# Joint steps for two query blocks of a key search and for two heads of a gated linear attention

## The chip, the cores and the metric

The kernel runs on one core of one Trainium2 chip. A core has a matrix engine (TensorE, PE in the profile), a vector engine (VectorE, DVE), a scalar engine (ScalarE, ACT), GpSimd (POOL) and a queue engine for DMAs (SyncE, SP). Each works through its own list of instructions in the order in which it was built, and waits on semaphores where an instruction needs what another engine makes. The metric is the device time of one execution, in microseconds (us); less is better.

## The reference

One layer of an encoder for 1024 tokens of width 1024, in float32: half a SwiGLU feed-forward step, a layer norm, a token mixer, a layer norm, another half feed-forward step, a layer norm. The mixer holds what the change touches:

```python
proj = h @ w_in                        # one projection, cut into groups of columns
# gated linear attention (GLA), 4 heads, in chunks: b is the running sum of the log gates
A = einsum('bhid,bhjd,bhijd->bhij', qn, kn, exp(b_i - b_j))   # causal
o = A @ v + (qn * exp(b)) @ S          # then a norm per head and a gate
# indexer attention (DSA), 8 heads: every query keeps its 256 best keys
score = einsum('bqh,bqhs->bqs', w, relu(q_idx . k_idx))       # admissible keys only
_, idx = lax.top_k(score, 256)
out = softmax over the kept keys
x = LN2(alpha * x + concat(o_gla, o_dsa) @ w_out)
```

## The kernel before

The mixer lies between the two feed-forward steps. Matrices are multiplied as a high and a low part, so each float32 product is three matmuls (L706 to L708, L723 to L725). A scheduler orders the instructions of each engine by a simulated timeline when the kernel is built; in the stretch below, the order of TensorE is pinned by hand (`in_order`, with a list that says how many projection steps follow each GLA step), while VectorE's, ScalarE's and GpSimd's follow from the simulation.

*Scores and search.* `index_scores` makes the scores of 128 queries (one block) against the keys up to them. Blocks 2 to 7 have more than 256 keys. `search_keys` finds each query's threshold bit by bit: a count of the scores above a trial threshold, a comparison of the count that gives 0 or a bit (`ge`), and a new threshold (`thr`), 32 times, one step waiting for the one before. Blocks 2 to 5 form one group: four counts on VectorE (L836), one comparison of four columns (L840), one update of four (L854). Blocks 6 and 7 are two groups of one block; their counts are ScalarE activations of 896 and 1024 columns (L833, with a row that reads the accumulator), their comparisons (L838) and updates (L852) single columns on VectorE. Then `keep_keys` turns a block's threshold into a mask on VectorE (L871 to L880; for blocks 6 and 7 `next_above`, L888 to L903, ahead of it); for blocks 5 and 6 it is held back until the third and fourth L1031.

*GLA.* `gla_pair` handles two of the four heads, pair 0 and then pair 1, and each in two halves of 512 tokens (i = 0, 1). A pair begins with the gates: pz by matmul (L937), L946, L951 and a running sum. A half begins with the diagonal: pd by matmul, then L1031 writes it into the tile `at` (128 x 1024). Then, for distances L = 64, 32, ..., 1, it scales keys and queries (ee by L1043, kz by GpSimd, qz by L1051), multiplies them (pa, L1057), and copies the result into `at` where a mask says so: on ScalarE for L = 64 (L1066), by a predicated copy for the others (L1068), once for each head. At last po = at · v + qe · state (L1082, L1085), the sum of squares (L1093, L1094) and the gated output og (L1098). The PSUM tiles pz, pd, pa and po come from two pools of two banks each, one per head.

*Beside it.* TensorE's time between GLA steps is filled with projections. In the second half of pair 1 these are `pf` (L706 to L708), each split by ScalarE (L1479) and VectorE (part, L1480) and sent to DRAM; two PSUM tiles take turns. After them attention begins (lg, L1149; e, L1153).

Of the kernel before, what the change touches and what calls it, by code (L numbers as in the profile page):

```python
# [7 lines left out]
F32 = mybir.dt.float32  # L8
# [107 lines left out]
class Block:  # L116
# [660 lines left out]
    def index_scores(self, b, parts, wI, ip, sp, ps, scores):  # L777

        nc = self.nc
        ik_hi, ik_lo, iq = parts  # L780
        n = (b + 1) * P
        sc = scores[b] = sp.tile([P, n], F32, name=f"score{b}")
        w = n if n <= 512 else n // 2
        for c0 in range(0, n, w):
            for h in range(8):
                pt = ps[h % 2].tile([P, 512], F32, tag="ps", name=self.uid("ps"))
                lhsT = iq[b // 4][h][:, b % 4 * P : (b % 4 + 1) * P]
                nc.tensor.matmul(pt[:, :w], lhsT, ik_hi[:, c0 : c0 + w], start=True, stop=False)
                nc.tensor.matmul(pt[:, :w], lhsT, ik_lo[:, c0 : c0 + w], start=False, stop=True)
                r = ip.tile([P, 512], F32, tag="relu", name=self.uid("relu"), bufs=2)  # L790
                nc.scalar.activation(r[:, :w], pt[:, :w], AF.Relu)
                if h == 0:
                    nc.vector.tensor_scalar(sc[:, c0 : c0 + w], r[:, :w], wI[:, b, 0:1], None, ALU.mult)
                else:
                    nc.vector.scalar_tensor_tensor(
                        sc[:, c0 : c0 + w], r[:, :w], wI[:, b, h : h + 1], sc[:, c0 : c0 + w], ALU.mult, ALU.add
                    )
                if h == 3:
                    yield
            yield  # L800
        nc.gpsimd.memset(sc[0:64, n - 64 : n], NEG)

    def search_keys(self, scores, keep, sp, tp):
# [12 lines left out]
        for gi, grp in enumerate(((2, 3, 4, 5), (6,), (7,))):  # L816
            s = {"blocks": grp, "act": gi >= 1, "id": gi, "n": (grp[-1] + 1) * P}
            t = keep.tile([P, 3, len(grp)], I32, name=f"search{gi}")
            s.update((k, t[:, j, :]) for j, k in enumerate(("ge", "thr", "cnt")))
            state.append(s)  # L820

        def count(s, value):

            count = s["cnt"].bitcast(F32)
            for j, b in enumerate(s["blocks"]):
                n = (b + 1) * P
                thr = s["thr"].bitcast(F32)[:, j : j + 1]
                cnt = count[:, j : j + 1]  # L830
                if s["act"]:
                    junk = tp.tile([P, 2 * T], BF16, tag="work", name=self.uid("junk"), bufs=1)
                    nc.scalar.activation(junk[:, :n], scores[b], AF.Sign, bias=thr, scale=-1.0, accum_out=cnt)  # L833
                else:
                    junk = sp.tile([P, s["n"]], U8, tag=f"junk{s['id']}", name=self.uid("junk"), bufs=1)
                    V.tensor_scalar(junk[:, :n], scores[b], thr, None, ALU.is_ge, ALU.add, accum_out=cnt)  # L836
            if s["act"]:
                V.tensor_scalar(s["ge"], count, float(s["n"] - 2 * TOPK + 1), value, ALU.is_le, ALU.mult)  # L838
            else:
                V.tensor_scalar(s["ge"], count, TOPK - 0.5, value, ALU.is_ge, ALU.mult)  # L840
# [6 lines left out]
        for p in range(30, -1, -1):  # L847
            for s in state:
                count(s, float(1 << p))
                xor = (ALU.bitwise_xor, ALU.bitwise_xor)  # L850
                if len(s["blocks"]) == 1:
                    V.tensor_scalar(s["thr"], s["thr"], turn[:, p : p + 1], s["ge"], *xor)  # L852
                else:
                    V.scalar_tensor_tensor(s["thr"], s["thr"], turn[:, p : p + 1], s["ge"], *xor)  # L854
# [52 lines left out]
    def gla_masks(self, pool):  # L907
# [9 lines left out]
        for s in range(6):  # L917
# [5 lines left out]
            masks[L] = self.const.tile([P, HP // L, L], U8, name=f"mask{L}")  # L923
# [3 lines left out]
    def gla_pair(self, p, g, gp, go, sgp, ps, masks, consts, o_dram):  # L927
# [6 lines left out]
        mz = kz  # L934
        for i in range(2):
            pz = ps[0].tile([P, 512], F32, tag="ps", name=self.uid("pz"))
            nc.tensor.matmul(  # L937
                pz,
                wa2[R_GA : R_GA + 16, p * P : (p + 1) * P],
                mT[R_GA : R_GA + 16, i * HT : (i + 1) * HT],  # L940
                start=True,
                stop=True,
                tile_position=(R_GA, 0),
            )
            nc.scalar.activation(az[i], pz, AF.Abs, bias=ba[:, p : p + 1], scale=1.0)
            V.tensor_scalar(mz[i], pz, ba[:, p : p + 1], 0.0, ALU.add, ALU.min)  # L946
# [60 lines left out]
        for i in range(2):  # L1007
# [6 lines left out]
            at = go.tile([P, 4, 2, P], F32, tag="at", name=self.uid("at"), bufs=1)  # L1014
            for step, L in enumerate((0, 64, 32, 16, 8, 4, 2, 1)):
# [7 lines left out]
                if L == 0:  # L1023
                    qk = kz[1]
                    nc.gpsimd.tensor_mul(qk, gk[:, ts], gq[:, ts])
                    pd = ps[0].tile([P, 8], F32, tag="ps", name=self.uid("pd"))
                    for j in range(4):
                        nc.tensor.matmul(
                            pd[:, 2 * j : 2 * j + 2], qk[:, j * P : (j + 1) * P], heads, start=True, stop=True
                        )  # L1030
                    V.tensor_mul(  # L1031
                        at.rearrange("p j h i -> p (j h) i"),
# [19 lines left out]
                pa = [t.tile([P, 4, HP], F32, tag="ps", name=self.uid("pa")) for t in ps]  # L1052
                m = HP if L == HP else P
                for j in range(4):
                    for h in range(2):
                        rows = slice(h * 64, h * 64 + 64)
                        nc.tensor.matmul(  # L1057
                            pa[h][:m, j, :],
# [5 lines left out]
                for h in range(2):  # L1064
                    if L == HP:
                        nc.scalar.activation(at[:HP, :, h, HP:], pa[h][:HP], AF.Copy)  # L1066
                    else:
                        V.copy_predicated(  # L1068
                            at[:, :, h, :].rearrange("p a (n s l) -> p a n s l", s=2, l=L)[:, :, :, 1, :],
                            masks[L].unsqueeze(1).to_broadcast([P, 4, HP // L, L]),  # L1070
                            pa[h].rearrange("p a (n l) -> p a n l", l=L),
                        )
# [3 lines left out]
            po = [t.tile([P, 4, P], F32, tag="ps", name=self.uid("po")) for t in ps]  # L1076
            for j in range(4):
                b = 4 * i + j
                tk = slice(j * P, (j + 1) * P)
                for h in range(2):  # L1080
                    vcols = slice(h * P, (h + 1) * P)
                    nc.tensor.matmul(po[h][:, j, :], at[:, j, h, :], gv[:, b, vcols], start=True, stop=(b == 0))  # L1082
# [151 lines left out]
    def run(self):  # L1234
# [15 lines left out]
        with tc.tile_pool(name="masks", bufs=1, reuse_waits="tile") as mkp:  # L1250
            masks = self.gla_masks(mkp)
# [169 lines left out]
        with ExitStack() as s2:  # L1421
# [8 lines left out]
            with ExitStack() as s3:  # L1430
                mp = s3.enter_context(tc.tile_pool(name="mix", bufs=1, reuse_waits="tile"))
                ps = [
                    s3.enter_context(tc.tile_pool(name=f"ps_mix{i}", bufs=2, space=PSUM, reuse_waits="tile"))
                    for i in range(2)
                ]
# [9 lines left out]

                s4 = ExitStack()
                ip = [s4.enter_context(tc.tile_pool(name="idx0", bufs=1, reuse_waits="tile"))]
# [44 lines left out]
                with s4:  # L1492
                    self.index_weights(mT, wI, 1)
                    side = dk_items()
                    for b in range(4, NB):
                        for _ in range(2):
                            next(side)
                        for _ in self.index_scores(b, parts, wI, ip[2], sp, ps, scores):
                            pass
                tp = s3.enter_context(tc.tile_pool(name="topk", bufs=1, reuse_waits="tile"))  # L1500
# [94 lines left out]
                for b in scores:  # L1595
# [74 lines left out]
        with ExitStack() as st, ExitStack() as ff_stack:  # L1670
# [3 lines left out]
            gb = xp.tile([P, 4, KD], F32, name="ln2_gb")  # L1674
# [116 lines left out]
```

## Time and profile before

| | |
|---|---|
| median of three runs | 1987.3 us (1987.25 to 1990.45) |
| profiled execution | 1987.65 us, span 1985.9 us |
| granted TensorE clock, mean of the span | 0.991 |
| busy: TensorE, VectorE, ScalarE, GpSimd | 97%, 76%, 42%, 32% |
| search and GLA pair 0 | about 811 to 964 us |
| GLA pair 1 | about 960 to 1092 us |

The profiled execution is 1.75 us longer than its span, which is what lies around the profile's first and last instruction. A row of the groups gives line, engine, operation, what is written and read, the shapes, the count, then busy time and mean nanoseconds of one, then the idle time of the engine ahead of it with what ended it. A row of the waits gives who waited for whom, the total, the number and the longest. A row of the timeline gives start, length, engine, line and operation, with idle time ahead of it in brackets. A length runs to the end of the instruction; the next one on the same engine can start a little earlier.

### The profile page before, as it was taken

Reading aid. Unit: us, or ns where it says so; the run is one execution under the profiler, and the core shown is the slowest. Engines: PE = TensorE matmul, PEld = TensorE weight load, DVE = VectorE, ACT = ScalarE, POOL = GpSimd, SP = SyncE. Lnnn points to the kernel's source line nnn. Section 1 sums busy time; section 2 is a strip of 40 time slices with the busy share of each in tenths; the row PEclk is TensorE's granted clock in tenths of the full one; section 3 lists DMA queues with packets and bytes.
Section 4 is the critical chain, followed back from the end, with each engine's and each line's share of the span. In section 5 each row is a group of like instructions: output and inputs, shape, how many; then the busy total and the mean of one; then the engine's idle time right before and its main releaser. Section 6 shows DMA issues by size and latency. Waiting matters only on the chain. (4 is left out here: it accounts for less than half of the span.)

```text
span 1985.9 us, 26695 instructions
## 1 busy us (share of the span) xinstructions
PE 1933.7 (97%) x9576; PEld 1584.2 (80%) x9576; DVE 1514.1 (76%) x2325; ACT 838.4 (42%) x1380; POOL 644.3 (32%) x531
## 2 busy tenths in 40 slices
PE   9999999999999999999899899999999999999996
PEld 7788888888888788777687678788888888888885
DVE  8777877775578768899967567478778878868677
ACT  5333323334334345798552456255332332234331
POOL 5454454430001102144343000025445444539011
PEclk9999999999999999998999899999999999999998
DMA  5454454478656222022115631523444534586663
GB/s 180 145 190 148 148 186 152 146 245 313 201 170 209 96 85 85 22 65 64 43 37 179 183 96 39 182 105 111 143 149 158 176 133 150 184 294 236 223 203 136
DMA packets 198309, 298.44 MB, mean 150 GB/s; under 512 B 18832, under 2 KB 102944, under 8 KB 198176
## 3 DMA queue, kind: packets, MB, share of 16 engines
q1 hardware_dynamic: 194272, 291.49, 44.8%
q10 hardware_dynamic: 3264, 3.15, 0.5%
q0 software_dynamic: 640, 2.10, 0.4%
q8 instruction: 75, 1.23, 0.3%
q14 instruction: 58, 0.48, 0.1%
HBM read 205.97 MB, written 90.70 MB: 149 GB/s over the span
## 5 line engine op out<-in xcount | busy, mean ns | idle before, releaser
L97 DVE TENSOR_TENSOR wloq<-rw,whiq 128x512 fp32r<-128x512 f32 (+2 forms) x211 | 212.9, 1010 | 126.2 <-ACT whiq L96 124.9
L97 DVE TENSOR_TENSOR wlod<-rd,whid 128x1024 fp32r<-128x1024 f32 x154 | 203.5, 1342 | 112.8 <-ACT whid L96 112.4
L96 ACT ACTIVATE whid<-rd 128x1024 fp32r<-128x1024 f32 x154 | 161.3, 1060 | 238.3 <-PE pd L543 122.1
L96 ACT ACTIVATE whiq<-rw 128x512 fp32r<-128x512 f32 (+2 forms) x211 | 164.2, 798 | 207.3 <-POOL rw L351 99.6
L543 PE MATMUL pd<-wlod,whid 128*128 128x512 f32 x616 | 239.6, 389 | 0.8 <-DVE wlod L97 0.8
L543 PE MATMUL pd<-whid,wlod 128*128 128x512 f32 x616 | 239.3, 389 | 0.0
L543 PE MATMUL pd<-whid 128*128 128x512 f32 x616 | 237.9, 390 | 0.0
L369 PE MATMUL pq<-b_h,whiq 128*128 128x512 f32 x576 | 226.3, 393 | 2.3 <-DVE c L418 1.8
L371 PE MATMUL pq<-b_h,wloq 128*128 128x512 f32 x576 | 225.5, 391 | 0.5 <-DVE wloq L97 0.5
L370 PE MATMUL pq<-b_l,whiq 128*128 128x512 f32 x576 | 225.4, 391 | 0.0
L228 POOL TENSOR_TENSOR rs<-ve,neghalf 128x1 f32<-128x1 f32 x24 | 34.2, 1427 | 473.9 <-DVE ve L252 322.1
L483 ACT ACTIVATE c<-c 128x512 f32<-128x512 f32 x80 | 50.7, 634 | 269.3 <-DVE c L405 182.3
L370 PE MATMUL pq<-xl,whiq 128*128 128x512 f32 x352 | 137.3, 390 | 0.6 <-DVE xl L97 0.6
L371 PE MATMUL pq<-xh,wloq 128*128 128x512 f32 x352 | 137.1, 389 | 0.0
L369 PE MATMUL pq<-xh,whiq 128*128 128x512 f32 x352 | 137.1, 389 | 0.0
L543 PEld LDWEIGHTS pd<-wlod,whid 128*128 128x128 f32 x616 | 115.7, 188 | 24.9 <-DVE wlod L97 1.1
L543 PEld LDWEIGHTS pd<-whid,wlod 128*128 128x128 f32 x616 | 115.6, 188 | 24.3
L543 PEld LDWEIGHTS pd<-whid 128*128 128x128 f32 x616 | 115.6, 188 | 23.9 <-ACT whid L96 0.2
L723 PE MATMUL pt<-whi,xh 128*128 128x512 f32 x320 | 131.0, 410 | 3.2 <-ACT stage L1550 1.6
L369 PEld LDWEIGHTS pq<-b_h,whiq 128*128 128x128 f32 x576 | 108.3, 188 | 26.6 <-DVE c L418 2.2
L371 PEld LDWEIGHTS pq<-b_h,wloq 128*128 128x128 f32 x576 | 108.1, 188 | 24.6 <-DVE wloq L97 1.0
L725 PE MATMUL pt<-whi,xl 128*128 128x512 f32 x320 | 127.7, 400 | 0.0
(275 smaller groups left out, 4533.8 us busy)
## 6 DMA issues: line engine op xcount, KB each, us to landing
rw<-in_ffn_w_gu_dram SPq DMA_DIRECT2D x87, 512.0 KB, 4.1
rd<-h_dram SPq DMA_DIRECT2D x154, 256.0 KB, 3.6
h_dram<-c SPq DMA_DIRECT2D x148, 256.0 KB, 2.9
rt<-in_ffn_w_down_dram SPq DMA_DIRECT2D x44, 512.0 KB, 3.4
t_dram<-rt SPq DMA_DIRECT2D x44, 512.0 KB, 2.9
rd<-t_dram SPq DMA_DIRECT2D x88, 256.0 KB, 3.7
rd<-in_ffn_w_down_dram SPq DMA_DIRECT2D x66, 256.0 KB, 4.8
raw<-in_w_in_dram SPq DMA_DIRECT2D x20, 512.0 KB, 3.7
```

The costliest lines, as they stand in the source:

```text
L96: self.nc.scalar.activation(hi, src, AF.Copy)
L97: self.nc.vector.tensor_sub(lo, src, hi)
L228: self.nc.gpsimd.tensor_tensor(dst, src, self.neghalf[:, :n], ALU.pow)
L369: mm(bank, wh[:, k, :], xh[:, k, :], start=start, stop=False)
L370: mm(bank, wh[:, k, :], xl[:, k, :], start=False, stop=False)
L371: mm(bank, wl[:, k, :], xh[:, k, :], start=False, stop=stop)
L483: nc.scalar.activation(t, t, AF.Silu)
L543: nc.tensor.matmul(bank, left, right, start=(i == 0 and n == 0), stop=(i == ng - 1 and n == 2))
L723: nc.tensor.matmul(pt, xh[:, k, cols], wh[:, k % 2, :], start=(k == 0), stop=False)
L725: nc.tensor.matmul(pt, xl[:, k, cols], wh[:, k % 2, :], start=False, stop=(k == KD - 1))
```

## The change

In the search, blocks 6 and 7 become one group on ScalarE. Its counts are both 1024 columns wide: block 6's score tile gets 128 more columns that GpSimd fills with the lowest value. A step is then two counts, one comparison and one update of two columns. In the GLA, both heads' PSUM tiles become one tile of two banks, from a pool of two such tiles, and `at` is laid out by head first; the copy of L = 64 on ScalarE and the predicated copies on VectorE take both heads at once (512 columns, 24 copies for 48). pz, too, is one tile for both halves, with both matmuls ahead of the steps that read it. The scores get a PSUM pool of their own that is closed before the GLA's opens. The masks are built at the mixer's start and kept in its pool, not at the program's start.

VectorE then has 2102 instructions for 2191 and ScalarE 1228 for 1234; TensorE has the same 8886, of which those of pair 0 stand in another order among the projections. The lines from `search_keys` on are numbered 3 to 5 higher: L836, L838, L840, L852 and L854 become L841, L843, L845 and (both) L856; L1031, L1057, L1068, L1098 and L1480 become L1035, L1062, L1072, L1103 and L1483.

```diff
-        sc = scores[b] = sp.tile([P, n], F32, name=f"score{b}")
+        sc = sp.tile([P, T if b == 6 else n], F32, name=f"score{b}")
+        scores[b] = sc[:, :n]
+        if b == 6:
+            nc.gpsimd.memset(sc[:, n:], NEG)
+            scores["wide", b] = sc
...
-        for gi, grp in enumerate(((2, 3, 4, 5), (6,), (7,))):
+        for gi, grp in enumerate(((2, 3, 4, 5), (6, 7))):
             s = {"blocks": grp, "act": gi >= 1, "id": gi, "n": (grp[-1] + 1) * P}
-            t = keep.tile([P, 3, len(grp)], I32, name=f"search{gi}")
+            t = keep.tile([P, 4, 4], I32, name=f"search{gi}")[:, :3, : len(grp)]
...
-                    nc.scalar.activation(junk[:, :n], scores[b], AF.Sign, bias=thr, scale=-1.0, accum_out=cnt)
+                    wide = scores["wide", 6] if b == 6 else scores[b]
+                    nc.scalar.activation(junk[:, :T], wide, AF.Sign, bias=thr, scale=-1.0, accum_out=cnt)
...
-                if len(s["blocks"]) == 1:
-                    V.tensor_scalar(s["thr"], s["thr"], turn[:, p : p + 1], s["ge"], *xor)
-                else:
-                    V.scalar_tensor_tensor(s["thr"], s["thr"], turn[:, p : p + 1], s["ge"], *xor)
+                V.scalar_tensor_tensor(s["thr"], s["thr"], turn[:, p : p + 1], s["ge"], *xor)
...
-            masks[L] = self.const.tile([P, HP // L, L], U8, name=f"mask{L}")
+            masks[L] = kept.tile([P, HP // L, L], U8, name=f"mask{L}")
...
+        pair = ps.tile([P, 2, 512], F32, tag="ps", name=self.uid("pz"))
         for i in range(2):
-            pz = ps[0].tile([P, 512], F32, tag="ps", name=self.uid("pz"))
             nc.tensor.matmul(
-                pz,
+                pair[:, i, :],
                 wa2[R_GA : R_GA + 16, p * P : (p + 1) * P],
                 mT[R_GA : R_GA + 16, i * HT : (i + 1) * HT],
                 start=True,
                 stop=True,
                 tile_position=(R_GA, 0),
             )
+        for i in range(2):
+            pz = pair[:, i, :]
...
-            at = go.tile([P, 4, 2, P], F32, tag="at", name=self.uid("at"), bufs=1)
+            at = go.tile([P, 2, 4, P], F32, tag="at", name=self.uid("at"), bufs=1)
...
-                    pd = ps[0].tile([P, 8], F32, tag="ps", name=self.uid("pd"))
+                    pd = ps.tile([P, 2, 512], F32, tag="ps", name=self.uid("pd"))[:, 0, :8]
...
-                pa = [t.tile([P, 4, HP], F32, tag="ps", name=self.uid("pa")) for t in ps]
+                pa = ps.tile([P, 2, 512], F32, tag="ps", name=self.uid("pa"))[:, :, : 4 * HP]
+                pa = pa.rearrange("p h (a l) -> p h a l", a=4)
...
-                for h in range(2):
-                    if L == HP:
-                        nc.scalar.activation(at[:HP, :, h, HP:], pa[h][:HP], AF.Copy)
-                    else:
-                        V.copy_predicated(
-                            at[:, :, h, :].rearrange("p a (n s l) -> p a n s l", s=2, l=L)[:, :, :, 1, :],
-                            masks[L].unsqueeze(1).to_broadcast([P, 4, HP // L, L]),
-                            pa[h].rearrange("p a (n l) -> p a n l", l=L),
-                        )
+                if L == HP:
+                    nc.scalar.activation(at[:HP, :, :, HP:], pa[:HP], AF.Copy)
+                else:
+                    V.copy_predicated(
+                        at.rearrange("p h a (n s l) -> p h a n s l", s=2, l=L)[:, :, :, :, 1, :],
+                        masks[L].unsqueeze(1).unsqueeze(1).to_broadcast([P, 2, 4, HP // L, L]),
+                        pa.rearrange("p h a (n l) -> p h a n l", l=L),
+                    )
...
-            po = [t.tile([P, 4, P], F32, tag="ps", name=self.uid("po")) for t in ps]
+            pair = ps.tile([P, 2, 512], F32, tag="ps", name=self.uid("po"))
+            po = [pair[:, h, :].rearrange("p (j f) -> p j f", j=4) for h in range(2)]
...
-        with tc.tile_pool(name="masks", bufs=1, reuse_waits="tile") as mkp:
-            masks = self.gla_masks(mkp)
...
-                ps = [
-                    s3.enter_context(tc.tile_pool(name=f"ps_mix{i}", bufs=2, space=PSUM, reuse_waits="tile"))
-                    for i in range(2)
-                ]
...
+                with tc.tile_pool(name="masks", bufs=1, reuse_waits="tile") as mkp:
+                    masks = self.gla_masks(mkp, mp)
...
+                ps = s4.enter_context(tc.tile_pool(name="ps_idx", bufs=4, space=PSUM, reuse_waits="tile"))
...
+                ps = s3.enter_context(tc.tile_pool(name="ps_gla", bufs=2, space=PSUM, reuse_waits="tile"))
...
-                for b in scores:
+                for b in range(TOPK // P, NB):
```

More of the change, by code (lines that the diff above doesn't have):

```diff
@@ L785, in index_scores @@
             for h in range(8):
-                pt = ps[h % 2].tile([P, 512], F32, tag="ps", name=self.uid("ps"))
+                pt = ps.tile([P, 512], F32, tag="ps", name=self.uid("ps"))
                 lhsT = iq[b // 4][h][:, b % 4 * P : (b % 4 + 1) * P]
@@ L903, in next_above, with gla_masks @@
         V.copy_predicated(tau, more, low)
-    def gla_masks(self, pool):
+    def gla_masks(self, pool, kept):
         nc = self.nc
@@ L1025, in gla_pair @@
                     nc.gpsimd.tensor_mul(qk, gk[:, ts], gq[:, ts])
-                    pd = ps[0].tile([P, 8], F32, tag="ps", name=self.uid("pd"))
+                    pd = ps.tile([P, 2, 512], F32, tag="ps", name=self.uid("pd"))[:, 0, :8]
                     for j in range(4):
                         nc.tensor.matmul(
-                            pd[:, 2 * j : 2 * j + 2], qk[:, j * P : (j + 1) * P], heads, start=True, stop=True
+                            pd[:, j::4], qk[:, j * P : (j + 1) * P], heads, start=True, stop=True
                         )
                     V.tensor_mul(
-                        at.rearrange("p j h i -> p (j h) i"),
+                        at.rearrange("p h j i -> p (h j) i"),
                         self.ident.unsqueeze(1).to_broadcast([P, 8, P]),
@@ L1057, in gla_pair @@
                         nc.tensor.matmul(
-                            pa[h][:m, j, :],
+                            pa[:m, h, j, :],
                             kk[rows, j * P : j * P + m],
@@ L1081, in gla_pair @@
                     vcols = slice(h * P, (h + 1) * P)
-                    nc.tensor.matmul(po[h][:, j, :], at[:, j, h, :], gv[:, b, vcols], start=True, stop=(b == 0))
+                    nc.tensor.matmul(po[h][:, j, :], at[:, h, j, :], gv[:, b, vcols], start=True, stop=(b == 0))
                 if b > 0:
@@ L1673, in run @@
             lp = ln_stack.enter_context(tc.tile_pool(name="ln2", bufs=1, reuse_waits="tile"))
-            gb = xp.tile([P, 4, KD], F32, name="ln2_gb")
+            gb = xp.tile([P, P], F32, name="ln2_gb")[:, : 2 * KD].rearrange("p (i k) -> p i k", i=2)
             self.affine = [gb[:, i, :] for i in range(2)]
```

## The prediction

> **What bounds the kernel now.** I read the page's first rows, then the busy time of each engine in stretches of 50 us, then the waits of TensorE in the stretches that are not full.
>
> ```profile
> span 1985.9 us, 26695 instructions
> PE 1933.7 (97%) x9576; PEld 1584.2 (80%) x9576; DVE 1514.1 (76%) x2325; ACT 838.4 (42%) x1380; POOL 644.3 (32%) x531
> ```
>
> TensorE (PE) is busy for 97% of the span. No row above changes its instructions, so the time can move only through its 52 us of gaps and through its clock. The stretches say where those lie (columns: stretch, length, then busy us and count of PE, PEld, DVE, ACT and POOL, the granted clock, the DMA share, GB/s):
>
> ```profile
> 850.00:900.00 50.00, 46.16 (x272) 36.89 (x271) 48.81 (x153) 45.23 (x79) 25.21 (x29) 0.93 0.21 64
> 900.00:950.00 50.00, 45.66 (x303) 37.61 (x302) 49.28 (x163) 42.50 (x88) 23.52 (x27) 0.93 0.25 75
> 950.00:1000.00 50.00, 43.93 (x218) 33.64 (x216) 48.85 (x105) 24.72 (x53) 16.92 (x17) 0.97 0.12 32
> 1000.00:1050.00 50.00, 48.50 (x320) 39.60 (x320) 31.60 (x61) 26.54 (x55) 25.35 (x29) 1.00 0.21 69
> ```
>
> From 850 to 1000 us VectorE (DVE) is full, at 48.8 to 49.3 us in 50, and TensorE lacks 3.8, 4.3 and 6.1 us. That is the search beside the first GLA pair and the entry of the second. From 1000 us VectorE has 18 us in 50 to spare and TensorE runs nearly without a stop. TensorE's longer waits from 850 to 1104 us:
>
> ```profile
> PE lg L1149 <- DVE mx L1153: 6.7, 1, 6.7
> PE pa L1057 <- DVE qz L1051: 4.0, 4, 1.5
> PE pa L1057 <- DVE at L1031: 3.9, 2, 2.6
> PE po L1082 <- DVE at L1068: 2.7, 1, 2.7
> PE pf L706 <- DVE part L1480: 1.4, 1, 1.4
> ```
>
> The wait at L1031 has its longest case at the entry of pair 1, that at L1480 in the second half of pair 1, and that of 6.7 us where attention begins.
>
> **The change part by part.** The durations of what is removed (groups of VectorE, then of ScalarE, from 811 to 1100 us; mean ns of one after the busy time):
>
> ```profile
> L1068 DVE COPY_PREDICATED at<-mask,pa 128x256 f32<-128x256 uint8 x48 | 23.1, 540 | 6.5 <-PE pa L1057 6.5
> L852 DVE TENSOR_SCALAR search<-search,turn 128x1 int32<-128x1 int32 x62 | 16.6, 269 | 0.0
> L838 DVE TENSOR_SCALAR search<-search 128x1 int32<-128x1 f32 x64 | 9.5, 149 | 4.8 <-ACT junk L833 4.5
> L854 DVE SCALAR_TENSOR_TENSOR search<-search,turn 128x4 int32<-128x4 int32 x25 | 7.9, 316 | 0.3
> L833 ACT ACTIVATE junk<-score,search 128x1024 bf16<-128x1024 f32 x32 | 36.7, 1145 | 9.0 <-DVE search L852 3.5 <-DVE search L838 3.2 <-POOL score L801 2.1
> L833 ACT ACTIVATE junk<-score,search 128x896 bf16<-128x896 f32 x31 | 32.2, 1038 | 3.2 <-DVE search L852 1.8 <-DVE search L838 1.2
> ```
>
> *VectorE's saving.* 64 of L838 become 32 of two columns, at the same 0.149 each: 4.8 us. 62 of L852 become 31 of L854's kind, at 0.316 or less: 16.6 − 9.8 = 6.8 us. Ends of these overlap the next start, so some 8 of the 11.6 us count as time. The joint copy of 512 columns has no row. If a copy's 0.540 were all fixed, 24 of 48 would save 13 us; if it were all by the column, nothing. Consecutive pairs below lie in 0.65 us (52.39 to 53.04), hence 0.33 from start to start; the nearest row with 512 columns, L1480 below, takes 0.60 (1049.80 to 1050.40). So I take 0.6 for a joint copy and 0.05 to 0.1 saved per pair, 1 us in pair 0. So pair 0's VectorE work falls by 9 us, with 5 and 15 as the ends.
>
> [...]
>
> *ScalarE.* 32 counts are widened by 128 columns: 32 × 0.108 = 3.5 us, less a few table loads. By its busy time (42%) this is nothing. But before, blocks 6 and 7 were two groups that took turns: while VectorE made the next threshold of one, ScalarE counted the other. Now both counts wait for one threshold and both must end before the next. The end of the search before:
>
> ```profile
> 948.37 1.05 ACT L833 ACTIVATE junk<-score,search 128x896 bf16<-128x896 f32 x1 [0.39 <-DVE search L838]
> 949.55 1.15 ACT L833 ACTIVATE junk<-score,search 128x1024 bf16<-128x1024 f32 x1
> 950.61 0.19 ACT L833 ACTIVATION_READ_ACCUMULATOR junk<-score,search 128x1 f32 x1
> 963.41 0.22 DVE L854 SCALAR_TENSOR_TENSOR search<-search,turn 128x4 int32<-128x4 int32 x1
> 992.50 1.21 DVE L1031 TENSOR_TENSOR at<-ident,pd 128x1024 f32<-128x1024 f32 x1
> ```
>
> ScalarE was done with its 32 steps at 950.8 us, 12.8 us ahead of VectorE's own group (963.6). A round of the new group is two counts (948.37 to 949.55 and 949.55 to 950.8, the first 0.1 longer at 1024 columns: 2.5 us) and two small VectorE steps (0.15 + 0.3): 2.9 us. VectorE's order at the end of the search, where L843 is the comparison (L838 before) and L856 the new threshold (L852, L854 before) of search_8698, the ScalarE group, and search_8697 is VectorE's own:
>
> ```order
> L841 TENSOR_SCALAR junk_9203,search_8697<-score_6060,search_8697 128x768
> L856 SCALAR_TENSOR_TENSOR search_8698<-search_8698,turn 128x2
> L845 TENSOR_SCALAR search_8697<-search_8697 128x4
> L856 SCALAR_TENSOR_TENSOR search_8697<-search_8697,turn 128x4
> L843 TENSOR_SCALAR search_8698<-search_8698 128x2
> L856 SCALAR_TENSOR_TENSOR search_8698<-search_8698,turn 128x2
> L1072 COPY_PREDICATED at_7335<-mask_5190,pa_7505 128x512
> ```
>
> L843 and L856 then follow four times more. Before, the same place held only VectorE's own group, and the keys of block 2 (L871) came straight after its last threshold:
>
> ```order
> L836 TENSOR_SCALAR junk_9327,search_8757<-score_6063,search_8757 128x768
> L840 TENSOR_SCALAR search_8757<-search_8757 128x4
> L854 SCALAR_TENSOR_TENSOR search_8757<-search_8757,turn 128x4
> L871 TENSOR_SCALAR keep_9339,above_9340<-score_5570,search_8757 128x384
> L872 TENSOR_SCALAR keep_9339<-score_5570,search_8757 128x384
> ```
>
> Five rounds of ScalarE's group stand after VectorE's last own threshold, with hardly any work between: the last copy of pair 0 after the first of them, one L950 (0.66 us, L946 before) before the last. VectorE takes them in order and waits at each. Its own group ends about 963.6 − 9 (saved) − 5 × 0.45 (steps still to come) = 952.4 us. The copy comes after one wait of 2.1 us and two steps, near 955.6 us, about where it stood before; so TensorE's 2.7 us for it (po at L1068) stays. Then the other rounds last until 952.4 + 2.6 + 4 × 2.9 = 966.6, and the keys of block 2 begin 3.0 us later than the 963.6 of before, with 0.7 us of later work done: L1031 of pair 1 ends about 2 us later. TensorE waits for it already (2.6), so **+2 us**, from −4 (15 us saved) to +6 (5 saved). All of VectorE's saving goes into waits for ScalarE.
>
> [...]
>
> *A move that the diff doesn't show.* In the second half of pair 1 TensorE computes projections (pf), each in one of two PSUM tiles, and the third must wait until VectorE's L1480 (L1483 in the changed kernel) has read the first. VectorE before, from 1037 us, with TensorE's row under it:
>
> ```profile
> 1037.09 1.22 DVE L1031 TENSOR_TENSOR at<-ident,pd 128x1024 f32<-128x1024 f32 x1 [0.55 <-PE pd L1028]
> 1043.63 2.15 DVE L1098 SCALAR_TENSOR_TENSOR og<-po,grs,gg 128x128 f32<-128x128 f32 x8
> 1045.70 0.67 DVE L1480 TENSOR_TENSOR part<-pf,part 128x512 fp32r<-128x512 f32 x1
> 1046.30 0.20 DVE L903 COPY_PREDICATED_SCALAR search<-na_more,na_low 128x1 f32 x1
> 1046.42 0.59 DVE L1051 TENSOR_TENSOR qz<-gq,ee 128x256 f32<-128x256 f32 x1
> 1046.94 0.68 DVE L1043 TENSOR_TENSOR ee<-bT 128x512 f32<-128x512 f32 x1
> 1047.54 1.13 DVE L871 TENSOR_SCALAR_CACHE_REDUCE keep<-score,search 128x896 f16<-128x896 f32 x1
> 1048.60 0.68 DVE L872 TENSOR_SCALAR keep<-score,search 128x896 f16<-128x896 f32 x1
> 1049.20 0.68 DVE L1043 TENSOR_TENSOR ee<-bT 128x512 f32<-128x512 f32 x1
> 1049.80 0.68 DVE L1480 TENSOR_TENSOR part<-pf,part 128x512 fp32r<-128x512 f32 x1
> 1050.40 0.14 DVE L874 TENSOR_SCALAR left<-above 128x1 f32<-128x1 f32 x1
> 1050.46 2.01 DVE L875 TENSOR_TENSOR_SCAN keep<-one,keep 128x896 f16<-128x896 f16 x1
> 1052.39 0.75 DVE L1068 COPY_PREDICATED at<-mask,pa 128x256 f32<-128x256 uint8 x2
> 1053.04 0.41 DVE L1051 TENSOR_TENSOR qz<-gq,ee 128x256 f32<-128x256 f32 x1
> 1053.37 1.14 DVE L876 SCALAR_TENSOR_TENSOR keep<-keep,left 128x896 f16<-128x896 f16 x1
> ```
>
> ```profile
> 1046.43 0.50 PE L706 MATMUL pf<-xh,whi 128*128 128x512 f32 x1 [1.41 <-DVE part L1480]
> ```
>
> The second head's og and the keys of block 6 stood behind L1480 or just ahead of it in the order before:
>
> ```order
> L1098 SCALAR_TENSOR_TENSOR og_8214<-po_8176,grs_8221,gg_7619 128x128 x4
> L1098 SCALAR_TENSOR_TENSOR og_8229<-po_8177,grs_8236,gg_7619 128x128 x4
> L1480 TENSOR_TENSOR part_8258<-pf_8169,part_8257 128x512
> L903 COPY_PREDICATED search_8758<-na_more_9389,na_low_9387 128x1
> L1051 TENSOR_TENSOR qz_6514<-gq_7616,ee_8370 128x256
> ```
>
> In the changed order, with the same steps renumbered (L1103 is og, L905, L1055, L1047 and L873 to L878 are L903, L1051, L1043 and L871 to L876), they stand between the first og and L1483:
>
> ```order
> L1103 SCALAR_TENSOR_TENSOR og_8169<-po_8132,grs_8176,gg_7589 128x128 x4
> L1047 TENSOR_TENSOR ee_8360<-bT_7562 128x512
> L905 COPY_PREDICATED search_8698<-na_more_9263,na_low_9261 128x1
> L1055 TENSOR_TENSOR qz_6516<-gq_7586,ee_8321 128x256
> L873 TENSOR_SCALAR keep_9266,above_9267<-score_6230,search_8698 128x896
> L874 TENSOR_SCALAR keep_9266<-score_6230,search_8698 128x896
> L877 SCALAR_TENSOR_TENSOR keep_9266<-one,keep_9266 128x896
> L1099 TENSOR_SCALAR ss_8183<-ss_8183 128x4
> L878 SCALAR_TENSOR_TENSOR keep_9266<-keep_9266,left_9270 128x896
> L1103 SCALAR_TENSOR_TENSOR og_8184<-po_8132,grs_8191,gg_7589 128x128 x4
> L1483 TENSOR_TENSOR part_8213<-pf_8125,part_8212 128x512
> ```
>
> All that stood behind L1480 from 1046.30 to 1052.39, less the 0.60 of the second L1480, is now ahead: 5.5 us; with it L876, some 1.1 us of its 1.14. That is 6.6 us. The second og needs a GpSimd step on ss that now lies right ahead, so up to 0.7 us more. TensorE's own order there is as before, and it already waited 1.41 us: **+6.9 us**, with 6.2 and 7.6 as ends; nothing earlier moves it, since VectorE's L1031 starts the count and itself waits for TensorE (0.55).
>
> A wait of over 8 us has a second cost, read from the stretch after the longest wait of before:
>
> ```profile
> 1099.00:1103.00 4.00, 3.96 (x15) 2.68 (x16) 2.06 (x15) 2.65 (x11) 0.00 (x0) 0.50 0.31 122
> 1103.00:1108.00 5.00, 5.00 (x37) 3.75 (x38) 3.73 (x23) 3.08 (x13) 0.00 (x0) 0.79 0.23 65
> ```
>
> The granted clock was 0.50 for 4 us and 0.79 for 5: 3.0 us lost. Part of it hides, as VectorE is then the later one for the next PSUM tile: the keys of block 7 stand ahead of the third L1483. I take **+2.3 us**, from 1 to 3.
>
> *Attention.* Its first reduction waited 5.4 us for a DMA out of kz, since its buffer shared addresses with kz; the moved masks shift it clear, but the second head's still overlaps. Three small matmuls can go ahead: **−1 us**, from 0 to −2. The masks' build now falls where VectorE idles before a weight arrives (about 440 us), at nothing; had it no cover it would cost some 2 us. The padding of block 6 is one GpSimd memset.
>
> Sum: +2 + 6.9 + 2.3 − 1 = +10.2 us on the profiled 1987.65 us, which is 0.35 over the median: 1987.3 + 10.2 = 1997.5 us.
>
> **The rivals.** *The saving holds (faster).* VectorE is full from 850 to 1000 us; if ScalarE's group kept pace, L1031 of pair 1 would come 9 us earlier. TensorE could use at most its waits there, 14.2 us, and would take about 9, so 1978; with the projection's wait in place 1986. It decides if a round takes under 2 us; against it stand two counts at 1.15. *A tie.* The two waits lie as forecast but the low ends meet: 15 us saved before the five rounds (−4), 6.2 at L1483, 1 for the clock, −2 at attention: +1.2, so 1988.5. For it: VectorE's saving has no row of its own, and 13 of the 15 us would need copies whose cost is all fixed; the spacing of 0.33 speaks against that. *More than I forecast.* The five rounds cost 3.4 us each instead of 2.9, and block 7's keys hold the third L1483 by 3 us too: +6, 2003. *The change doesn't do what it says*: joint copies could run as two halves, 24 × 0.1 = 2.4 us more on VectorE; it lies inside the ends above.
>
> **How the numbers follow.** Chances: forecast 0.68 (1992 to 2001 by its own ends), more than that 0.12, tie 0.12, faster 0.08. The likeliest gives 1997.5 us. The range reaches from 1986 (the saving holds, with the projection's wait) to 2004 (the upper case). A measurement of this kernel can tell about 0.2%, 4 us, from no change. So faster 0.08, same 0.12, slower 0.80.
>
> **What would show it.** Right: in the changed profile VectorE idles 2 us or so at L843 five times between 950 and 968 us, with ScalarE's L833 (L838) as releaser; TensorE waits 8 us at L706 for L1483 near 1046 us, and the clock falls after it; attention's wait is about 1 us shorter. Wrong: L843 finds its counts ready, or L1483 runs within 9 us of the last L1035, and then the time is at or below 1987.

## The result, and the profile after

The changed kernel took 2009.13 us (median of four runs, 2008.64 to 2010.1) against 1987.75 us before in the same runs: a ratio of 1.0106, with a 95% interval of 1.0093 to 1.0118. It is slower by 21.4 us, where 10.2 were forecast. The page of the profile after:

```profile
span 2007.3 us, 26558 instructions
PE 1934.9 (96%) x9576; PEld 1590.1 (79%) x9576; DVE 1509.2 (75%) x2236; ACT 840.3 (42%) x1374; POOL 636.3 (32%) x532
```

TensorE's work is what it was, and its busy time too (1934.9 us for 1933.7), so most of the 21 us show as new gaps. The same stretches as before:

```profile
850.00:900.00 50.00, 44.88 (x250) 34.19 (x248) 45.27 (x113) 43.74 (x68) 23.80 (x28) 1.00 0.23 69
900.00:950.00 50.00, 40.35 (x276) 33.50 (x277) 49.61 (x128) 38.66 (x78) 22.53 (x25) 0.83 0.16 48
950.00:1000.00 50.00, 41.71 (x188) 32.88 (x186) 34.30 (x85) 37.20 (x71) 16.82 (x19) 0.90 0.20 53
1000.00:1050.00 50.00, 48.60 (x323) 39.82 (x323) 33.12 (x52) 24.27 (x46) 21.81 (x22) 1.00 0.07 22
```

From 900 to 950 us VectorE is still full (49.6) and TensorE has lost five more us and clock (0.83). From 950 to 1000 us VectorE is no longer full: 34.3 us in 50, and TensorE waits all the same. TensorE's longest waits now, from 850 us to the start of attention:

```profile
PE pf L706 <- DVE part L1483: 9.6, 1, 9.6
PE pa L1062 <- DVE qz L1055: 6.5, 3, 4.5
PE pa L1062 <- DVE at L1035: 4.4, 2, 3.0
PE pt L723 <- ACT gk L1529: 3.8, 2, 3.0
PE po L1087 <- DVE at L1072: 3.3, 1, 3.3
```

The first is the wait for the projection's PSUM tile that stood at 1.4 us; the fourth is a wait for ScalarE that was not there. The longest wait for the diagonal (L1035) is now in pair 0, 3.0 us; at pair 1's entry it is 1.4, where 2.6 stood.

Both kernels have 9576 matmuls, and from the end of pair 0 on in one order but for pair 1's two gate matmuls. So the k-th matmul from the end is the same piece of work in both, and the difference of its start times says how much had been lost by then. This ledger (us after the time of the kernel before, at the place that stands at that time before) is worked out from the profiled execution of every kernel in this study:

| kernel | 962: end of pair 0 | 980: pair 1's entry | 1036: its second half | 1052: after the projection's wait | 1128: attention | 1397: second feed-forward | end |
|---|---|---|---|---|---|---|---|
| the change | 10.4 | 16.8 | 12.7 | 25.1 | 26.3 | 26.2 | 21.4 |
| gb_pad | 0.1 | 0.1 | 0.1 | 0.2 | 0.6 | 0.2 | −4.6 |
| search_only | 5.1 | 13.0 | 7.5 | 7.9 | 7.6 | 7.5 | 7.5 |
| two_groups | 2.1 | 6.3 | 6.0 | 18.1 | 18.2 | 17.9 | 13.1 |
| late_keys | 10.5 | 12.8 | 13.7 | 23.0 | 23.4 | 22.9 | 18.8 |
| squares_first | 11.1 | 12.3 | 14.3 | 14.4 | 15.2 | 14.7 | 9.9 |
| squares_gates_first | 3.8 | 5.1 | 6.9 | 7.0 | 6.8 | 6.3 | 1.5 |
| two_groups_reads_first | −1.1 | −1.1 | 2.4 | 2.8 | 4.5 | 4.1 | −0.7 |
| single_columns | 4.4 | 10.8 | 5.7 | 18.6 | 19.0 | 18.5 | 13.7 |
| gb_256 | 0.9 | 0.9 | 1.1 | 1.1 | 0.5 | 0.1 | −4.6 |
| reads_first_single | 4.5 | 3.7 | 0.8 | 0.8 | 1.5 | 1.0 | −3.8 |

The first row splits the 21.4 us: 12.7 until pair 1's second half, of which 10.4 stand by the end of pair 0, 12.4 at the projection's wait, 1.2 at attention, and 4.8 won back in the second feed-forward step. The forecast put pair 0 at nothing and named no term in the second feed-forward step.

The end of the search, VectorE after (the thresholds of its own group end with the first row; L843 is the comparison of ScalarE's group, L873 starts the keys of block 2):

```profile
960.04 0.22 DVE L856 SCALAR_TENSOR_TENSOR search<-search,turn 128x4 int32<-128x4 int32 x1
962.57 0.17 DVE L843 TENSOR_SCALAR search<-search 128x2 int32<-128x2 f32 x1 [2.31 <-ACT junk L838]
962.91 1.32 DVE L1072 COPY_PREDICATED at<-mask,pa 128x512 f32<-128x512 uint8 x1
965.64 0.17 DVE L843 TENSOR_SCALAR search<-search 128x2 int32<-128x2 f32 x1 [1.41 <-ACT junk L838]
969.99 0.57 DVE L843 TENSOR_SCALAR search<-search 128x2 int32<-128x2 f32 x1 [3.93 <-ACT junk L838]
973.90 0.17 DVE L843 TENSOR_SCALAR search<-search 128x2 int32<-128x2 f32 x1 [2.64 <-ACT junk L838]
977.65 0.17 DVE L843 TENSOR_SCALAR search<-search 128x2 int32<-128x2 f32 x1 [0.38 <-ACT junk L838]
977.72 0.61 DVE L873 TENSOR_SCALAR_CACHE_REDUCE keep<-score,search 128x384 f16<-128x384 f32 x1
```

The five waits are there. But VectorE's own group ends at 960.3 us, not at 952.4, and the rounds last 3.1, 4.4, 3.9 and 3.8 us, not 2.9. ScalarE in the second of them shows why: its own list puts other work between the two counts.

```profile
966.16 1.15 ACT L838 ACTIVATE junk<-score,search 128x1024 bf16<-128x1024 f32 x1 [0.55 <-DVE search L856]
967.31 1.04 ACT L72 ACTIVATE whi<-raw 128x1024 fp32r<-128x1024 f32 x1
968.26 0.57 ACT L1529 ACTIVATE gq<-pf 128x512 f32<-128x512 f32 x1
968.73 1.13 ACT L838 ACTIVATE junk<-score,search 128x1024 bf16<-128x1024 f32 x1
```

The second place is pair 1's second half. VectorE, then ScalarE (L1098 is the square of an output of po, four for each head):

```profile
1049.81 1.22 DVE L1035 TENSOR_TENSOR at<-ident,pd 128x1024 f32<-128x1024 f32 x1 [0.51 <-PE pd L1032]
1056.76 1.11 DVE L1103 SCALAR_TENSOR_TENSOR og<-po,grs,gg 128x128 f32<-128x128 f32 x4
1063.75 0.14 DVE L1099 TENSOR_SCALAR ss<-ss 128x4 f32<-128x4 f32 x1
1065.92 1.13 DVE L1103 SCALAR_TENSOR_TENSOR og<-po,grs,gg 128x128 f32<-128x128 f32 x4 [0.91 <-POOL grs L228]
1066.96 0.68 DVE L1483 TENSOR_TENSOR part<-pf,part 128x512 fp32r<-128x512 f32 x1
```

```profile
1050.22 0.28 ACT L1098 ACTIVATE sq<-po 128x128 bf16<-128x128 f32 x1
1058.34 0.28 ACT L1098 ACTIVATE sq<-po 128x128 bf16<-128x128 f32 x1 [2.27 <-DVE og L1103]
1060.81 0.27 ACT L1098 ACTIVATE sq<-po 128x128 bf16<-128x128 f32 x1
```

The fourth square of the first head starts at 1050.22; the first of the second head only at 1058.34, released by VectorE's first output. Its sum, its output and L1483 follow one after the other.

### The profile page after: what moved, and what is told of

Same layout as the page of the kernel before. It is cut to its first block, busy times and chain, and to the rows that moved or that the text cites. A ratio compares the mean times of both kernels' runs of the same rounds, so it can differ in the third digit from the quotient of the medians.

```text
span 2007.3 us, 26558 instructions
## 1 busy us (share of the span) xinstructions
PE 1934.9 (96%) x9576; PEld 1590.1 (79%) x9576; DVE 1509.2 (75%) x2236; ACT 840.3 (42%) x1374; POOL 636.3 (32%) x532
## 5 line engine op out<-in xcount | busy, mean ns | idle before, releaser
L228 POOL TENSOR_TENSOR rs<-ve,neghalf 128x1 f32<-128x1 f32 x24 | 30.0, 1251 | 477.6 <-DVE ve L252 325.5
L724 PE MATMUL pt<-wlo,xh 128*128 128x512 f32 x320 | 128.2, 400 | 0.0
```

The lines of the kernel that those rows point to most:

```text
L228: self.nc.gpsimd.tensor_tensor(dst, src, self.neghalf[:, :n], ALU.pow)
L724: nc.tensor.matmul(pt, xh[:, k, cols], wl[:, k % 2, :], start=False, stop=False)
```

## The experiments

Each was run beside the kernel before on the same chip; the times of before were 1988.33 us in the first four runs below, 1988.35 in the next four and 1988.55 in the last two.

**gb_pad**, on the kernel before:

```diff
-            gb = xp.tile([P, 4, KD], F32, name="ln2_gb")
+            gb = xp.tile([P, P], F32, name="ln2_gb")[:, : 2 * KD].rearrange("p (i k) -> p i k", i=2)
```

> The kernel before with one edit: the tile of LN2's gains takes 512 bytes a partition in place of 128, as in the change. Alignment theory (the tiles after it start at another place in a 512-byte line, and the matmuls of the second feed-forward step that read b_h and t1h then go from 229.7 ns to 226.7 ns): 4 to 5 us faster, about 1983, with the whole gain between the second layer norm and 1735 us. Rival (the gain in that stage comes from a later start, since DMA or the clock differs): 1987.7, no change.

1983.77 us, ratio 0.9979 (0.9969 to 0.9989). In the ledger nothing moves up to 1397 us, and then 4.8 us are won. One stretch of 100 us in that stage, before, after the change, and with this edit alone:

```profile
1500.00:1600.00 100.00, 100.00 (x437) 81.69 (x436) 77.57 (x84) 33.33 (x50) 45.46 (x30) 1.00 0.45 154
```

```profile
1500.00:1600.00 100.00, 100.00 (x443) 82.81 (x442) 78.56 (x85) 30.63 (x47) 50.33 (x34) 1.00 0.42 143
```

```profile
1500.00:1600.00 100.00, 100.00 (x443) 82.81 (x442) 76.17 (x85) 33.21 (x50) 45.16 (x30) 1.00 0.47 160
```

TensorE is full at clock 1.00 in all three, but 437 matmuls start before and 443 with the edit. The change makes the same edit, in a line that its diff above leaves out, so the 4.8 us that it wins back come from there.

**two_groups**, the change without its search part:

```diff
-        for gi, grp in enumerate(((2, 3, 4, 5), (6, 7))):
+        for gi, grp in enumerate(((2, 3, 4, 5), (6,), (7,))):
...
-                    nc.scalar.activation(junk[:, :T], wide, AF.Sign, bias=thr, scale=-1.0, accum_out=cnt)
+                    nc.scalar.activation(junk[:, :n], scores[b], AF.Sign, bias=thr, scale=-1.0, accum_out=cnt)
```

> The change without its search part: blocks 6 and 7 are two ScalarE groups again, with 896 and 1024 columns and single-column steps. Theory A (the search's single chain on ScalarE costs the 16 us by which pair 1 begins later; the joint copies cost little; the late read of the projection costs 12 us): pair 1's second half begins within 3 us of before, the wait for the projection's PSUM tile stays at 8 to 10 us, the second feed-forward step gains 5; together 1993 to 1997. Theory B (the joint PSUM tiles and copies delay pair 0): 2005 or more. Theory C (only the search grouping moved the late read): 1983 to 1988.

2001.62 us, ratio 1.0066 (1.0052 to 1.0080): between theory A's and B's numbers. The wait for the projection is there in full (12 us in the ledger), so it belongs to the joint tiles and not to the search. But 6 us are lost before it as well, which A did not allow.

**search_only**, the search part of the change on the kernel before (the same lines the other way, the wide score tile, the joint update and the moved masks):

```diff
-        for gi, grp in enumerate(((2, 3, 4, 5), (6,), (7,))):
+        for gi, grp in enumerate(((2, 3, 4, 5), (6, 7))):
```

> The kernel before with the search part alone (one group of blocks 6 and 7, 1024 columns; the masks are moved to make room), copies by head. Theory A: 10 to 16 us are lost by the start of pair 1, no long wait for the projection's PSUM tile, no gain in the second feed-forward step: 1998 to 2004. Theory B: 1987 to 1990. Theory C (the grouping alone brings the late read): 2010 or more.

1994.09 us, ratio 1.0027 (1.0016 to 1.0037). No long wait, no gain in the second feed-forward step, as A and the run above say; but 7.5 us lost by the ledger (5.8 by the medians) and not 10 to 16. The two parts do not add up to the change (7.5 and 6.0 until pair 1's second half, 12.7 together), but nearly.

**late_keys**, the change with block 6's keys held back:

```diff
                     nc.vector.tensor_sub(part[1], pt, part[0])
+                    self.split.append(nc.cur_bb.bb.instructions[-1])
...
-                    with self.behind(self.begun[b - 7], mybir.EngineType.DVE) if b in (5, 6) else ExitStack():
+                    first = {5: self.begun[-2], 6: self.split[8]}.get(b)
+                    with self.behind(first, mybir.EngineType.DVE) if first else ExitStack():
```

> The change with one more dependency: VectorE begins the keys of block 6 after the first low part of the projection in pair 1's second half, not after that half's diagonal. If the late read is what costs there, the wait of 9.6 us falls to 0 to 2, the clock stays up after it, and the time falls by 10 to 12 us to 1997 to 1999. Rival (VectorE has so much work in that half that TensorE waits later for another step): 2003 to 2009.

2005.88 us, ratio 1.0086 (1.0070 to 1.0101). TensorE's wait falls from 9.6 to 7.1 us only, though the keys are out of the way: VectorE then stands idle ahead of the second head's sum.

```profile
1059.26 0.69 DVE L1048 TENSOR_TENSOR ee<-bT 128x512 f32<-128x512 f32 x1
1062.68 0.17 DVE L1100 TENSOR_SCALAR ss<-ss 128x4 f32<-128x4 f32 x1 [2.73 <-ACT sq L1099]
1063.98 1.13 DVE L1104 SCALAR_TENSOR_TENSOR og<-po,grs,gg 128x128 f32<-128x128 f32 x4 [1.12 <-POOL grs L229]
1065.02 0.68 DVE L1484 TENSOR_TENSOR part<-pf,part 128x512 fp32r<-128x512 f32 x1
```

So the keys cost 2.5 us, and for the rest they were filling time that was lost anyway. The run's time lies in the rival's range, but VectorE is idle there, not full. My theory of the late read falls here as the main cause; the squares become the suspect (theory D in the next expectations).

**squares_first**, the change with all squares written ahead of the outputs:

```diff
-            for h in range(2):
-                ss = go.tile([P, 4], F32, tag="ss", name=self.uid("ss"), bufs=2)
-                og = sgp.tile([P, 4, P], F32, tag=f"og{h}", name=self.uid("og"))
+            sums = []
+            for h in range(2):
+                ss = go.tile([P, 4], F32, tag="ss", name=self.uid("ss"), bufs=2)
                 sq = go.tile([P, P], BF16, tag="sq", name=self.uid("sq"), bufs=1)
                 for j in range(4):
                     nc.scalar.activation(sq, po[h][:, j, :], AF.Square, accum_out=ss[:, j : j + 1])
+                sums.append(ss)
+            for h in range(2):
+                ss = sums[h]
+                og = sgp.tile([P, 4, P], F32, tag=f"og{h}", name=self.uid("og"))
```

> The change with the squares of both heads (L1098, ScalarE) written ahead of both heads' outputs (L1103, VectorE), as they ran before. Theory D (po is now one tile, so ScalarE's reads of the second head stand behind VectorE's reads of the first, and with them the second output and the read of the projection): the wait for the projection's PSUM tile falls from 9.6 to 1 to 3 us, the clock stays up, and the time falls by 10 to 12 us to 1997 to 1999. Rival (VectorE's other work, the keys of block 6, holds the read): 2006 to 2009.

1996.40 us, ratio 1.0043 (1.0028 to 1.0058): 12.7 us less than the change. ScalarE's first and last square, VectorE from the diagonal to the read, and TensorE's only listed wait in that stretch:

```profile
1050.58 0.28 ACT L1098 ACTIVATE sq<-po 128x128 bf16<-128x128 f32 x1 [0.24 <-PE po L1090]
1053.38 0.28 ACT L1098 ACTIVATE sq<-po 128x128 bf16<-128x128 f32 x1
```

```profile
1051.37 1.22 DVE L1035 TENSOR_TENSOR at<-ident,pd 128x1024 f32<-128x1024 f32 x1 [0.50 <-PE pd L1032]
1057.96 2.15 DVE L1107 SCALAR_TENSOR_TENSOR og<-po,grs,gg 128x128 f32<-128x128 f32 x8
1060.03 0.68 DVE L1487 TENSOR_TENSOR part<-pf,part 128x512 fp32r<-128x512 f32 x1
```

```profile
PE pf L706 <- DVE part L1487: 1.4, 1, 1.4
```

All eight squares run in one go, both outputs follow, and the read comes 8.7 us after the diagonal as before the change (8.6), with the same wait of 1.4. Theory D holds: with both heads in one tile, ScalarE's reads of the second bank had come to stand behind VectorE's reads of the first.

**squares_gates_first**: the same for pz, which is also one tile now.

```diff
             nc.scalar.activation(az[i], pz, AF.Abs, bias=ba[:, p : p + 1], scale=1.0)
-            V.tensor_scalar(mz[i], pz, ba[:, p : p + 1], 0.0, ALU.add, ALU.min)
+        for i in range(2):
+            V.tensor_scalar(mz[i], pair[:, i, :], ba[:, p : p + 1], 0.0, ALU.add, ALU.min)
```

> As the run with the squares first, and also both of ScalarE's reads of pz ahead of VectorE's reads. Theory D: another 2 to 4 us less at the entry of pair 1, 1994 to 1996. Rival (the entry is late only because the search ends late): the same as the run with the squares first.

1988.55 us, ratio 1.0006 (0.9997 to 1.0015): another 7.9 us less, twice what theory D expected. The ledger has 7.3 of them by the end of pair 0. There ScalarE made the first pair's gates from 856.3 to 870.4 us with four table loads in squares_first, and from 856.8 to 866.5 us with two here. The pattern is easier to see in pair 1, which comes too late for the 7.3 us. In the change ScalarE had its gates like this:

```profile
975.80 0.68 ACT L949 ACTIVATE az<-pz,ba 128x512 f32<-128x512 f32 x1
977.76 0.64 ACT L952 ACTIVATE az<-az 128x512 f32<-128x512 f32 x1
978.28 0.69 ACT L949 ACTIVATE az<-pz,ba 128x512 f32<-128x512 f32 x1
979.48 1.28 ACT L954 ACT_TABLE_LOAD   x1
981.42 1.28 ACT L952 ACT_TABLE_LOAD   x1
983.37 1.28 ACT L954 ACT_TABLE_LOAD   x1
```

The second half's |pz| comes 2.5 us after the first's, since VectorE reads the first in between (976.52). The first half then goes through its exponential and its logarithm alone, and ScalarE loads its tables three times. TensorE's wait of 3.0 us for gk (L1529) lies behind these. How much of the 7.9 us is the gates and how much the new order of the whole of pair 0 was not taken apart.

**two_groups_reads_first**: two_groups with both edits of the reads.

> The joint copies and PSUM tiles without the search part, with ScalarE's reads of po and pz ahead of VectorE's. If theory D is all that the joint tiles cost: no long wait for the projection, pair 1's second half begins within 3 us of before, the second feed-forward step gains 5: 1982 to 1986, equal to or under the kernel before. If the joint tiles cost pair 0 as well: 1987 to 1991.

1985.99 us, ratio 0.9987 (0.9977 to 0.9996). Pair 1's second half begins 2.4 us after its time before, the second feed-forward step gives 4.8 back. The joint copies and PSUM tiles, their reads in order, lie 2 us above gb_pad (1983.77), which the two intervals do not keep apart; a saving is not to be seen.

**single_columns**, the change with the ScalarE group's small steps by the column:

```diff
-                V.tensor_scalar(s["ge"], count, float(s["n"] - 2 * TOPK + 1), value, ALU.is_le, ALU.mult)
+                for j in range(len(s["blocks"])):
+                    c = slice(j, j + 1)
+                    V.tensor_scalar(s["ge"][:, c], count[:, c], float(s["n"] - 2 * TOPK + 1), value, ALU.is_le, ALU.mult)
...
-                V.scalar_tensor_tensor(s["thr"], s["thr"], turn[:, p : p + 1], s["ge"], *xor)
+                        V.tensor_scalar(s["thr"][:, c], s["thr"][:, c], turn[:, p : p + 1], s["ge"][:, c], *xor)
```

> The change with one ScalarE group, but its comparison and its new threshold are made column by column, as 128x1 steps of the kind that L838 and L852 were. Contention theory (two-column steps are held while GpSimd runs, at 0.5 to 0.7 us for 0.17 to 0.22, and single ones are not): VectorE's own group ends no later than in the change though it has 63 more steps, and the time is 2000 to 2007. Serial theory (the chain through ScalarE sets the end): 2009 to 2013.

2000.44 us, ratio 1.0066 (1.0051 to 1.0081): 8.7 us less than the change, with 63 steps more on VectorE. The time lies in the contention theory's range, but VectorE's own group ended at 965.9 us, later than the change's 960.3, so the theory is not borne out in the form that it was written. What moved is ScalarE's chain: its last count ended at 952.1 us (977.5 in the change, 950.7 before). By 940 us it had made 29 of 32 rounds, as before; the change 24. With single columns the two blocks need not wait for each other, so this is two groups again in all but the width of the counts.

**gb_256**: gb_pad with `[P, 64]` in place of `[P, P]`.

> The kernel before with LN2's gains in 256 bytes a partition in place of 128, so that the second step's t1h lies 256 bytes off its weights in a 512-byte line, where it is 128 off before and 0 off with 512. If any shift does it, or the distance counts to 256 bytes: 1983 to 1984, as with 512. If the distance counts to 512 bytes: 1987 to 1989, as before.

1983.70 us, ratio 0.9975 (0.9966 to 0.9985), as with 512 bytes.

**reads_first_single**: squares_gates_first with the single columns.

> The change with ScalarE's reads of po and pz ahead of VectorE's, and the ScalarE group's small steps column by column. It lays bare what the two-column steps cost once the reads are in order: if they cost as they seem to (2.6 us between the two runs with the reads first), 1985 to 1987; if they cost more (8.7 us between the change and the run with single columns), 1979 to 1983, which would beat the kernel before with the 512-byte tile; if nothing, 1988 to 1990.

1982.92 us, ratio 0.9968 (0.9958 to 0.9979): faster than both kernels, and level with gb_pad. The two-column steps, with the order that follows from them, cost 5.6 us once the reads are in order. The three edits, of the squares (12.7), the gates (7.9) and the small steps (5.6), make 26.2 us together and so take away all of the 25.4 by which the change lies above gb_pad.

## Why the prediction was wrong

The sign was right, and so was the place of the projection's wait. The size was not: the term at pair 1's entry, +2 us, measured 12.7, mostly lost before that place, and the projection's term rested on the wrong cause.

*VectorE's saving, 9 us by the end of its own group.* The step that failed first is "some 8 of the 11.6 us count as time", and with it the end of VectorE's own group at 952.4 us. The groups of the small steps after, from 805 to 1115 us, and the joint copies:

```profile
L856 DVE SCALAR_TENSOR_TENSOR search<-search,turn 128x2 int32<-128x2 int32 x31 | 10.6, 342 | 0.1
L843 DVE TENSOR_SCALAR search<-search 128x2 int32<-128x2 f32 x32 | 8.0, 250 | 14.4 <-ACT junk L838 14.1
L1072 DVE COPY_PREDICATED at<-mask,pa 128x512 f32<-128x512 uint8 x24 | 22.0, 916 | 12.0 <-PE pa L1062 11.8
```

Busy time fell by 26.1 − 18.6 = 7.5 us, near the forecast, and the copies' by 1.1. But from start to start, waits left out, the single columns had taken only 17.0 us (0.08 and 0.19 each), since the next instruction starts under their ends, and the two-column ones took 11.8 for what of them ran by the end of the group. And part of the small steps had cost nothing: a count on VectorE that came straight after the accumulator read of the count before it started 0.12 us after that read, but a small step could start together with it (both at 958.66 us in the change, with the next count at 958.78). From 811 us to the end of the group 11 counts came straight after such a read before the change, and 40 after it: 3.4 us more. The joint copies saved under 0.4 us in pair 0 from start to start, not 1: for the last two distances a pair of copies took 1.1 us before, and so does a joint one. So the group ended 3.3 us earlier than before and not 11.

*The five rounds at 2.9 us, +2 us at pair 1.* The mechanism is there: VectorE does wait five times, 0.4 to 3.9 us. But the rounds took up to 4.4 us, since ScalarE's own list had weights, gates and squares between the counts; I took ScalarE to be free for them. The keys of block 2 began at 977.7 us and not at 966.6: 7.9 us of that come from the late end of VectorE's own group, 3.5 from the last four rounds. Then the gates of pair 1 came late (the reads of pz), which I had not seen. The diagonal that was to move by 2 us moved by 14.4, from 992.50 us:

```profile
1006.87 1.21 DVE L1035 TENSOR_TENSOR at<-ident,pd 128x1024 f32<-128x1024 f32 x1
```

TensorE's wait for it became shorter all the same (1.4 us for 2.6), since TensorE was late by then. Most of the 12.7 us had been lost ahead of the five rounds, in pair 0, which the sum put at nothing: its first po ran at 916.1 us for 908.7, and its last copy at 962.9 us, not near 955.6. Pair 0's gates stood later in TensorE's order (their first matmul at 856.2 us for 818.5), and ahead of the first diagonal VectorE waited for ScalarE's counts and gates four times between 852 and 878 us, 4.1 us in all, where 0.65 us stood in one wait. That diagonal moved from 875.75 us to:

```profile
882.47 1.21 DVE L1035 TENSOR_TENSOR at<-ident,pd 128x1024 f32<-128x1024 f32 x1
```

In search_only, with the PSUM tiles of before, the gates stand as late (855.4 us), so the joint group with its two-column steps brings that order. How the 10.4 us at the end of pair 0 divide between this order, the reads of pz and the two-column steps stays open, since each edit of the search or of the reads brought another order there.

*The projection's PSUM tile, +6.9 us.* It was 9.6 − 1.4 = 8.2 us, at the step named, but the cause failed: with "the keys of block 6" out of the way 7.1 − 1.4 = 5.7 of them stayed (late_keys). The order showed the second sum and output standing behind them, and I read them as moved with the rest; that sum could not have run earlier, because ScalarE's squares of the second head were held by VectorE's output of the first (squares_first).

*The clock, +2.3 us.* The ledger has 12.4 us at that place, hence 4.2 beyond the wait: the granted clock was 0.50 from 1067.7 to 1076 us. I had let part of it hide.

*Attention, −1 us.* It was +1.2. The first reduction no longer waits for the DMA out of kz (5.4 us before), but the second head's does (7.0 us), and TensorE waited 7.4 us in three pieces for 6.7 in one.

*Not in the sum.* The larger tile of LN2's gains was taken for bookkeeping. It gave 4.8 us back; without it the change would have cost some 26.

## What to carry to other kernels

Joining two tiles that two engines read joined their dependencies too: the edit of the squares' reads gave back 12.7 us, and the same for the gates 7.9, with a new order of pair 0. Write all reads of the one engine ahead of the other's, or keep the tiles apart, and look in the order for a reader that now stands behind the other engine's work. A small step that ran in another instruction's gap saved nothing when it went: a gap of 0.12 us between an accumulator read and the next count stood in its place, 40 times for 11. So price it from start to start and ask what starts in its place. Joining two serial chains saved 63 instructions on VectorE but made each wait for the other (24 of 32 rounds made by 940 us, where 29 had been). Count how many rounds the joined chain has left when its partner is done, and price a round with what else stands in that engine's list. When an order shows a read late, ask what is the last thing it needs, not only what stands ahead of it.

## What the runs showed of the hardware

*Where a matmul's operands lie.* In the second feed-forward step of the kernel before, t1h and b_h (and their low parts) start 128 bytes off their weights modulo 512, by the built kernels' addresses, and xh 0 bytes off; that addresses count modulo 512 was the author's assumption, and no run shows it. Their matmuls took 233 ns from start to start, with many at 238, those of xh 227; in the mean that is 229.7, and it is 226.7 where all starts are equal (the change, gb_pad). With 256 bytes between them (gb_256, 1983.70 us) it was as fast as with 0 (gb_pad, 1983.77); with 128 again in search_only, nothing was won (the ledger has 7.5 us at 1397 us and 7.5 at the end). So 128 bytes apart was slow here, and 0 or 256 was not; other distances were not run. The groups in the same stage, from 1400 to 1700 us, before and in gb_pad:

```profile
L369 PE MATMUL pq<-b_h,whiq 128*128 128x512 f32 x121 | 47.7, 395 | 0.0
```

```profile
L369 PE MATMUL pq<-b_h,whiq 128*128 128x512 f32 x122 | 47.5, 389 | 0.0
```

*Steps of two columns took longer beside GpSimd, steps of one did not.* In the change, VectorE's two-column update took 216 ns in the mean where GpSimd was idle at its start (23 times) and 706 where it was at work (8 times, of which one, beside a GpSimd step of four columns, was not longer), the two-column comparison 165 (24 times) and 505 (8 times). The single-column steps of the kernel before took 270 (42 times) and 268 (20 times), and 150 (45 times) and 147 (19 times). Two updates of the change in one row, of two and of four columns, without and with GpSimd at work, and GpSimd's row over the second:

```profile
934.71 0.33 DVE L856 SCALAR_TENSOR_TENSOR search<-search,turn 128x2 int32<-128x2 int32 x2
941.42 1.35 DVE L856 SCALAR_TENSOR_TENSOR search<-search,turn 128x2 int32<-128x2 int32 x2
```

```profile
938.79 6.06 POOL L75 TENSOR_TENSOR wlo<-raw,whi 128x256 fp32r<-128x256 f32 x8 [1.64 <-ACT whi L72]
```

The update's eight steps beside GpSimd took some 0.5 us more in the mean (706 − 216 ns), the comparison's eight 0.3 (505 − 165 ns); together that makes 6.6 us. Why the two-column steps took longer there and the single ones did not, no run shows. How much of the 5.6 us that the two-column steps cost is this, and how much that each block's count waits for the other's, the runs do not settle.
